# Loading the rows for the norm statistics two steps ahead of their squares, into the shared working tiles

## The chip, the cores and the metric

The kernel runs on one core of a Trainium2 chip. A core has five engines that run side by side, each through its own list of instructions in order: TensorE (matmuls; PE in the profile, its weight loads PEld), VectorE (DVE), ScalarE (ACT), GpSimd (POOL) and SyncE (SP), which here does little but issue DMAs. They wait for one another by semaphores. The metric is the time of one execution on the device in microseconds.

## The reference

The reference is one layer of a bidirectional encoder over 256 tokens of width 2048, in float32. Cut to what matters here:

```python
def rmsnorm(x, g):
    xf = x.astype(jnp.float32)
    y = xf * lax.rsqrt(jnp.mean(jnp.square(xf), axis=-1, keepdims=True) + EPS)
    return (y * g.astype(jnp.float32)).astype(x.dtype)
...
h = rmsnorm(x, norm_mix_g[l])
proj = h @ w_in[l]
...
qa = rmsnorm(split_heads(na_q, NA_HEADS), na_q_norm_g[l]) * (NA_HEAD_DIM ** -0.5)
...
mkv = rmsnorm(mem, mem_norm_g[l]) @ w_mem_kv[l]
```

Neighbourhood attention, retention and cross-attention into `mem` follow, each branch goes through a matrix of its own, the gated sum through `w_out`, and a squared-ReLU MLP ends the layer. The two norms of `x` and of `mem` need, for each token, the sum of the squares of its 2048 values.

## The kernel before

The work is a list of *units*. A unit is one tile of weights of 512 KB (two blocks of 128 rows, 512 columns) with its twelve matmuls of 512 columns: two blocks of rows, two halves of the tokens, and three products each (lines 101 to 103), since every operand is split into a high part and a low part that together carry float32. Eight units make a chunk of 512 output columns for `w_in`; the first three chunks are q and k of two head pairs twice, and v, then comes the same for the other heads, then the chunks of `w_mem_kv`.

For unit i the weights are loaded by SP into `raw` (line 242; five buffers, issued four units ahead), split by ScalarE into `w_hi` (line 94) and by VectorE into `w_lo` (line 95; four buffers each, split two units ahead in the program's text), and multiplied. For the first eight units the same happens to the transposed input: a load of `xT` into `xt_in` (line 160), and pieces `hT_hi` and `hT_lo` (lines 97 and 98).

The input is multiplied without the norm's factor, and the factor `r_x` is put in when a chunk is finished. So the statistics run beside the chunks, as a task: `stats_task` (line 167) loads the rows of `x`, 128 tokens by 512 columns (256 KB) at a time into `x_in`, and ScalarE squares them in place and leaves the sums in `ss` (line 175). After eight such blocks VectorE reduces `ss` (line 177), GpSimd raises to the power of -1/2 (lines 144 and 145), and VectorE makes one refining step (lines 146 to 149). The task for `x` is spawned at the start, that for `mem` (factor `r_m`) at unit 20.

`x_in` has a buffer of its own, one of it. Most other pieces of work take turns in twelve buffers of 2 KB per partition, the tag `t2`: `xt_in`, `qraw` (a finished chunk of q and k, copied from PSUM by ScalarE, line 300), `junk` (its squares, line 308), `na_bias`, `sb` (softmax rows), `pT`.

Behind `r_x` come, in this order: the squares of `qraw` on ScalarE (line 308), their sums on VectorE (line 309), the power on GpSimd, the normalising of `qraw` on VectorE (lines 320 and 322), its transposes on TensorE (line 287), and their split into `na_qkT` (lines 97 and 98). An attention head then makes scores `ps`, adds the bias and takes the maximum (line 379), exponentiates on ScalarE (line 357), scales (line 360), transposes (line 347) and multiplies by v.

The order on each engine is set by the tile framework's scheduler when the program is built. A buffer's next writer waits for its last reader; an instruction that waits holds up all behind it on its engine, and a DMA that waits holds up all behind it on SP.

Of the kernel before, what the change touches and what calls it, by code (L numbers as in the profile page):

```python
# [12 lines left out]
F32 = mybir.dt.float32  # L13
# [5 lines left out]
P = 128  # L19
D = 2048  # L20
S = 256
NT = S // P
KT = D // P
CW = 512
# [33 lines left out]
def encoder_layer(ctx: ExitStack, tc: tile.TileContext, a, out):  # L58
# [5 lines left out]
    wk = ctx.enter_context(tc.tile_pool(name="wk", bufs=12))  # L64
# [40 lines left out]
    def t2(name, dt=F32):  # L105

        return wk.tile([P, NT, S], dt, name=name, tag="t2")

    def t2f(name):
        return t2(name).rearrange("p t s -> p (t s)")  # L110
# [27 lines left out]
    def rsqrt_mean(ss, n, count, dst=None):  # L138

        u = st.tile([P, 8], F32, name="rs_u")  # L140
        y0 = st.tile([P, 8], F32, name="rs_y0")
        t = st.tile([P, 8], F32, name="rs_t")
        y = st.tile([P, 8], F32, name="rs_y") if dst is None else dst
        nc.gpsimd.tensor_scalar(u[:, :n], ss, 1.0 / count, EPS, op0=ALU.mult, op1=ALU.add)
        nc.gpsimd.tensor_tensor(y0[:, :n], u[:, :n], neg_half[:, :n], op=ALU.pow)
        nc.vector.tensor_tensor(t[:, :n], y0[:, :n], y0[:, :n], op=ALU.mult)
        nc.vector.tensor_tensor(t[:, :n], t[:, :n], u[:, :n], op=ALU.mult)
        nc.vector.tensor_scalar(t[:, :n], t[:, :n], -0.5, 1.5, op0=ALU.mult, op1=ALU.add)
        nc.vector.tensor_tensor(y[:, :n], y0[:, :n], t[:, :n], op=ALU.mult)
        return y  # L150
# [16 lines left out]
    def stats_task(src, dst):  # L167
        nh = D // CW
        ss = const.tile([P, NT, nh], F32, name=f"ss_{src.tensor.name}")
        for h in range(nh):  # L170
            for t in range(NT):
                xx = wk.tile([P, CW], F32, name="x_in", bufs=1)
                nc.sync.dma_start(xx, src[t * P:(t + 1) * P, h * CW:(h + 1) * CW])
                yield
                nc.scalar.activation(xx, xx, AF.Square, accum_out=ss[:, t, h:h + 1])
        s2 = st.tile([P, NT], F32, name="s2")
        nc.vector.tensor_reduce(s2, ss, axis=AX.X, op=ALU.add)
        rsqrt_mean(s2, NT, D, dst)
# [47 lines left out]
    raws, splits, x_in = {}, {}, []  # L226
# [301 lines left out]

    spawn(consts_task())
    spawn(stats_task(a["x"], r_x))  # L530

    memT = Lhs("memT")
# [392 lines left out]
    for i in range(n_units):  # L925
        issue(i + LOADS)
        do_split(i + SPLITS)
        for j in range(i, min(i + LEAD + 1, n_units)):
            if isinstance(units[j], Product):
                for lead, fn in units[j].acts:  # L930
                    if lead == j - i:
                        fn()
        if i == 20:
            spawn(stats_task(a["mem"], r_m))
        if i == 28:
            spawn(mem_task())
        if i == 100:
            spawn(decay_task())
        if i == u_out - 4:
            for c in range(4):  # L940
                env["x1", c] = quad_f("x1")
                nc.gpsimd.dma_start(env["x1", c],
                                    a["x"][:, c * CW:(c + 1) * CW].rearrange("(t p) d -> p t d", p=P))
        do_mm(i)
        units_done.append(i)
        run_tasks(i)
    i = n_units
# [105 lines left out]
```

## Time and profile before

| | |
|---|---|
| time, median of 3 runs | 1843.16 us (1839.11 to 1846.07) |
| the profiled execution's own time | 1837.19 us |
| its span, first to last instruction | 1835.4 us |
| TensorE busy | 1803.3 us, 98% of the span |
| VectorE busy | 1258.2 us, 69% |
| ScalarE busy | 977.5 us, 53% |
| GpSimd busy | 107.0 us, 6% |
| granted TensorE clock | 0.998 |
| bytes moved | 381.75 MB, 208 GB/s in the mean |

The durations below come from the one profiled execution, and all starts count from the start of its span. Busy time of TensorE is time with a matmul in flight; a matmul of 512 columns is shown as some 0.39 us long while the next one starts 0.23 us after it.

### The profile page before, as it was taken

The numbers are of one execution on the slowest core, as the hardware profiler recorded it, in microseconds if no ns is written. First come the engines' busy times: TensorE is split into PE (matmuls) and PEld (weight loads), VectorE is DVE, ScalarE is ACT, GpSimd is POOL, SyncE is SP. The second block draws the span as 40 slices with busy tenths as digits, with TensorE's granted clock in tenths as the row PEclk, the third lists the DMA queues.
The fourth block names the chain that finished last, engine by engine and source line by source line (L and its number), as shares of the span: only waits on it lengthen the run. The fifth ranks groups of instructions, "written<-read, shape, count | busy, mean of one in ns | idle before, by whom it ended". The sixth has DMA issues, their size and how long they took to land.

```text
span 1835.4 us, 22408 instructions
## 1 busy us (share of the span) xinstructions
PE 1803.3 (98%) x8248; PEld 1489.9 (81%) x8248; DVE 1258.2 (69%) x1608; ACT 977.5 (53%) x1222; POOL 107.0 (6%) x120
## 2 busy tenths in 40 slices
PE   8999999999999999999999999998999999999999
PEld 6778888888888888888888888776888887888887
DVE  5678766745454575675655555787888878888884
ACT  6566555544444444444444445955565656666562
POOL 0101010000000000000000000011101111110100
PEclk9999999999999999999999999999999999999999
DMA  8776455455555555545565555697888798979764
GB/s 269 261 228 209 161 173 172 164 193 194 195 189 198 188 170 185 172 162 195 187 213 197 193 184 183 197 258 209 243 261 237 239 269 233 260 242 273 212 208 144
DMA packets 131581, 381.75 MB, mean 208 GB/s; under 512 B 12176, under 2 KB 12688, under 8 KB 131472
## 3 DMA queue, kind: packets, MB, share of 16 engines
q1 hardware_dynamic: 114736, 346.07, 55.0%
q0 software_dynamic: 16448, 33.56, 10.1%
q8 instruction: 64, 1.05, 0.2%
q10 hardware_dynamic: 288, 0.70, 0.1%
q14 instruction: 45, 0.37, 0.1%
HBM read 378.19 MB, written 2.10 MB: 207 GB/s over the span
## 4 chain that ended last, share of the span: by engine, by line
PE 80%; DMA 10%; DVE 4%; ACT 3%; issue 2%; POOL 0%; SPq 0%; ACTq 0%; DVEq 0%; POOLq 0%
PE acc L102 23%; PE acc L101 23%; PE acc L103 23%; DMA b<-in_w_ff 6%; DVE w_lo L95 3%; PE ps L103 2%; PE ps L101 2%; PE ps L102 2%; ACT w_hi L94 2%; DMA x_in<-in_mem 2%; DMA x_in<-in_x 1%; DMA raw<-in_w_ff 1%; PE pt L103 1%; PE pt L101 1%; PE pt L102 1%
## 5 line engine op out<-in xcount | busy, mean ns | idle before, releaser
L95 DVE TENSOR_TENSOR w_lo<-raw,w_hi 128x1024 fp32r<-128x1024 f32 (+1 forms) x585 | 711.3, 1221 | 408.4 <-ACT w_hi L94 406.4
L94 ACT ACTIVATE w_hi<-raw 128x1024 fp32r<-128x1024 f32 (+1 forms) x585 | 616.2, 1057 | 540.8 <-PE acc L103 481.4
L101 PE MATMUL acc<-w_hi,hT_hi 128*128 128x512 f32 x1024 | 403.4, 394 | 7.1 <-ACT hT_hi L97 4.9
L102 PE MATMUL acc<-w_lo,hT_hi 128*128 128x512 f32 x1024 | 400.4, 391 | 4.5 <-DVE w_lo L95 4.5
L103 PE MATMUL acc<-w_hi,hT_lo 128*128 128x512 f32 x1024 | 399.7, 390 | 0.0
L94 ACT ACTIVATE w_hi<-b 128x1024 fp32r<-128x1024 f32 x140 | 148.1, 1062 | 175.0 <-DMA b<-in_w_ff 57.8
L101 PEld LDWEIGHTS acc<-w_hi,hT_hi 128*128 128x128 f32 x1024 | 192.9, 188 | 46.5 <-ACT hT_hi L97 4.9
L102 PEld LDWEIGHTS acc<-w_lo,hT_hi 128*128 128x128 f32 x1024 | 192.8, 188 | 44.8 <-DVE w_lo L95 6.8
L103 PEld LDWEIGHTS acc<-w_hi,hT_lo 128*128 128x128 f32 x1024 | 192.6, 188 | 40.7
L95 DVE TENSOR_TENSOR w_lo<-b,w_hi 128x1024 fp32r<-128x1024 f32 x140 | 169.5, 1222 | 78.0 <-ACT w_hi L94 76.7
L102 PE MATMUL acc<-w_lo,fT_hi 128*128 128x512 f32 x512 | 200.0, 391 | 2.4 <-DVE w_lo L95 2.4
L101 PE MATMUL acc<-w_hi,fT_hi 128*128 128x512 f32 x512 | 200.4, 391 | 0.3 <-DVE x L773 0.3
L103 PE MATMUL acc<-w_hi,fT_lo 128*128 128x512 f32 x512 | 199.4, 390 | 0.0
L102 PEld LDWEIGHTS acc<-w_lo,fT_hi 128*128 128x128 f32 x512 | 96.2, 188 | 23.9 <-DVE w_lo L95 4.3
L101 PEld LDWEIGHTS acc<-w_hi,fT_hi 128*128 128x128 f32 x512 | 96.3, 188 | 20.4 <-issue 0.7
L103 PEld LDWEIGHTS acc<-w_hi,fT_lo 128*128 128x128 f32 x512 | 96.2, 188 | 20.0
L819 POOL DMA_DIRECT2D b<-in_w_ff x56 | 68.1, 1363 | 549.1 <-DVE b L823 196.0
L101 PE MATMUL acc<-w_hi,memT_hi 128*128 128x512 f32 x128 | 50.8, 397 | 0.0
L101 PE MATMUL acc<-w_hi,mT_hi 128*128 128x512 f32 x128 | 50.6, 395 | 0.0
L102 PE MATMUL acc<-w_lo,memT_hi 128*128 128x512 f32 x128 | 50.0, 390 | 0.0
L103 PE MATMUL acc<-w_hi,memT_lo 128*128 128x512 f32 x128 | 50.0, 390 | 0.0
L103 PE MATMUL acc<-w_hi,mT_lo 128*128 128x512 f32 x128 | 49.9, 390 | 0.0
(266 smaller groups left out, 2439.2 us busy)
## 6 DMA issues: line engine op xcount, KB each, us to landing
raw<-in_w_in SPq DMA_DIRECT2D x255, 512.0 KB, 3.3
raw<-in_w_ff SPq DMA_DIRECT2D x200, 512.0 KB, 5.9
b<-in_w_ff SPq DMA_DIRECT2D x56, 512.0 KB, 7.0
b<-in_w_ff POOLq DMA_DIRECT2D x56, 512.0 KB, 8.9
raw<-in_w_mem_kv SPq DMA_DIRECT2D x32, 512.0 KB, 3.2
raw<-in_w_br_ret SPq DMA_DIRECT2D x32, 512.0 KB, 3.4
raw<-in_w_out SPq DMA_DIRECT2D x32, 512.0 KB, 3.2
raw<-in_w_br_na SPq DMA_DIRECT2D x16, 512.0 KB, 3.2
```

The costliest lines, as they stand in the source:

```text
L94: nc.scalar.activation(hi, src, AF.Copy)
L95: nc.vector.tensor_tensor(lo, src, f(hi), op=ALU.subtract)
L101: nc.tensor.matmul(o, lhsT=lh, rhs=rh, start=start, stop=False)
L102: nc.tensor.matmul(o, lhsT=lh, rhs=rl, start=False, stop=False)
L103: nc.tensor.matmul(o, lhsT=ll, rhs=rh, start=False, stop=stop)
L819: nc.gpsimd.dma_start(ring[n][k % 2].rearrange("p (b c) -> p b c", b=2), src, accum_op=ALU.add)
```

## The change

In `stats_task`, the blocks no longer go through a tile of their own but through the shared working tiles `t2`, and the square of a block is put two steps behind its load: at each step the next block is loaded, and the block of two steps ago is squared.

```diff
@@ -167,12 +167,17 @@
     def stats_task(src, dst):
         nh = D // CW
         ss = const.tile([P, NT, nh], F32, name=f"ss_{src.tensor.name}")
-        for h in range(nh):
-            for t in range(NT):
-                xx = wk.tile([P, CW], F32, name="x_in", bufs=1)
+        held = []
+        for i in range(nh * NT + 2):
+            if i < nh * NT:
+                h, t = i // NT, i % NT
+                xx = t2f("x_in")
                 nc.sync.dma_start(xx, src[t * P:(t + 1) * P, h * CW:(h + 1) * CW])
-                yield
+                held.append((xx, t, h))
+            if i >= 2:
+                xx, t, h = held.pop(0)
                 nc.scalar.activation(xx, xx, AF.Square, accum_out=ss[:, t, h:h + 1])
+            yield
         s2 = st.tile([P, NT], F32, name="s2")
         nc.vector.tensor_reduce(s2, ss, axis=AX.X, op=ALU.add)
         rsqrt_mean(s2, NT, D, dst)
```

All lines behind line 178 move down by five. With the scheduler the change moves instructions on every engine up to about unit 60; behind that the order is the same. TensorE's order is the same up to unit 36, but for the matmuls of unit 7 among themselves. Three places:

On SP, the loads of the first units, from the load of xT for unit 4 on, with what each waits for (DMAHW is an earlier DMA, Activation is ScalarE, DVE is VectorE). Before:

```order
L160 DMA xt_in<-in_xT 128x512 [waits DMAHW4_49]
L173 DMA x_in<-in_x 128x512 [waits DMAHW5_49]
L242 DMA raw<-in_w_in 128x1024 [waits DMAHW6_49,DVE_49]
L160 DMA xt_in<-in_xT 128x512 [waits DMAHW7_49]
L242 DMA raw<-in_w_in 128x1024 [waits DMAHW0_49,DVE_49]
L173 DMA x_in<-in_x 128x512 [waits DMAHW1_49,Activation_49]
L160 DMA xt_in<-in_xT 128x512 [waits DMAHW2_49]
L242 DMA raw<-in_w_in 128x1024 [waits DMAHW3_49,DVE_49]
L160 DMA xt_in<-in_xT 128x512 [waits DMAHW4_49]
L173 DMA x_in<-in_x 128x512 [waits DMAHW5_49,Activation_49]
```

And now:

```order
L160 DMA xt_in<-in_xT 128x512 [waits DMAHW4_49]
L175 DMA x_in<-in_x 128x512 [waits DMAHW5_49]
L247 DMA raw<-in_w_in 128x1024 [waits DMAHW6_49,DVE_49]
L160 DMA xt_in<-in_xT 128x512 [waits DMAHW7_49]
L175 DMA x_in<-in_x 128x512 [waits DMAHW0_49]
L247 DMA raw<-in_w_in 128x1024 [waits DMAHW1_49,DVE_49]
L160 DMA xt_in<-in_xT 128x512 [waits DMAHW2_49]
L175 DMA x_in<-in_x 128x512 [waits DMAHW3_49]
L247 DMA raw<-in_w_in 128x1024 [waits DMAHW4_49,DVE_49]
L160 DMA xt_in<-in_xT 128x512 [waits DMAHW5_49]
```

Each load of x now has no wait for ScalarE, and one stands with every weight load instead of every second one.

On VectorE, the first reduction of the statistics, counted from the last piece of hT (unit 7). Before, `x9` being nine splits in a row:

```order
L98 SCALAR_TENSOR_TENSOR hT_lo<-xt_in,c_gains,hT_hi 128x256 x2
L95 TENSOR_TENSOR w_lo<-raw,w_hi 128x1024 x9
L177 TENSOR_REDUCE s_370<-ss_in_x 128x2
L146 TENSOR_TENSOR rs_t<-rs_y_373 128x2
L147 TENSOR_TENSOR rs_t<-rs_t,rs_u 128x2
L148 TENSOR_SCALAR rs_t<-rs_t 128x2
L149 TENSOR_TENSOR r_x<-rs_y_373,rs_t 128x2
L95 TENSOR_TENSOR w_lo<-raw,w_hi 128x1024
L309 TENSOR_REDUCE ssq<-junk 128x4 x2
```

And now:

```order
L98 SCALAR_TENSOR_TENSOR hT_lo<-xt_in,c_gains,hT_hi 128x256 x2
L95 TENSOR_TENSOR w_lo<-raw,w_hi 128x1024 x4
L182 TENSOR_REDUCE s_406<-ss_in_x 128x2
L146 TENSOR_TENSOR rs_t<-rs_y_409 128x2
L147 TENSOR_TENSOR rs_t<-rs_t,rs_u 128x2
L148 TENSOR_SCALAR rs_t<-rs_t 128x2
L149 TENSOR_TENSOR r_x<-rs_y_409,rs_t 128x2
L77 COPY c_tables<-r_x 128x1
L95 TENSOR_TENSOR w_lo<-raw,w_hi 128x1024
L314 TENSOR_REDUCE ssq<-junk 128x4 x2
L95 TENSOR_TENSOR w_lo<-raw,w_hi 128x1024
L146 TENSOR_TENSOR rs_t<-rs_y_500 128x8
```

The reduction moved up by five units: it stands ahead of the split of unit 12 instead of unit 17, and the normalising behind it ahead of unit 14 instead of unit 19.

On VectorE, the reduction for mem. Before, the split behind it is that of unit 31:

```order
L95 TENSOR_TENSOR w_lo<-raw,w_hi 128x1024 x4
L98 SCALAR_TENSOR_TENSOR na_qkT_lo<-pt,c_gains,na_qkT_hi 128x2x128
L177 TENSOR_REDUCE s_868<-ss_in_mem 128x2
L146 TENSOR_TENSOR rs_t<-rs_y_871 128x2
L98 SCALAR_TENSOR_TENSOR na_qkT_lo<-pt,c_gains,na_qkT_hi 128x2x128
L147 TENSOR_TENSOR rs_t<-rs_t,rs_u 128x2
L148 TENSOR_SCALAR rs_t<-rs_t 128x2
L149 TENSOR_TENSOR r_m<-rs_y_871,rs_t 128x2
L95 TENSOR_TENSOR w_lo<-raw,w_hi 128x1024
```

And now, where the split behind it is that of unit 25:

```order
L95 TENSOR_TENSOR w_lo<-raw,w_hi 128x1024
L182 TENSOR_REDUCE s_931<-ss_in_mem 128x2
L146 TENSOR_TENSOR rs_t<-rs_y_934 128x2
L147 TENSOR_TENSOR rs_t<-rs_t,rs_u 128x2
L148 TENSOR_SCALAR rs_t<-rs_t 128x2
L149 TENSOR_TENSOR r_m<-rs_y_934,rs_t 128x2
L95 TENSOR_TENSOR w_lo<-raw,w_hi 128x1024 x2
L98 SCALAR_TENSOR_TENSOR v_lo<-acc_543,r_x,v_hi 128x512
```

The eight loads for mem follow on SP the weight loads of units 23 to 27 in ones and twos, where before they were spread over those of units 23 to 33.

## Rows read from the trace of the kernel before

**Rows 1.** Windows: stretch, length, PE, PEld, DVE, ACT, POOL busy, clock, DMA share, GB/s.

```profile
0.00:10.00 10.00, 3.31 (x6) 1.98 (x7) 3.83 (x18) 4.76 (x9) 0.68 (x6) 1.00 0.74 229
10.00:20.00 10.00, 10.00 (x42) 8.15 (x41) 9.83 (x21) 9.36 (x17) 0.00 (x0) 1.00 0.94 355
20.00:30.00 10.00, 10.00 (x45) 8.28 (x45) 6.25 (x10) 5.71 (x11) 0.00 (x0) 1.00 0.86 272
10.00:150.00 140.00, 132.77 (x611) 108.23 (x610) 95.59 (x186) 90.21 (x158) 15.76 (x19) 1.00 0.76 253
```

**Rows 2.** Tile x_in, its landing times; then SP's own waits to 110 us.

```profile
DMA to landing us min/median/max: 3.1/4.1/7.3
...
SPq L173 <- ACT x_in L175: 38.7, 13, 4.5
```

**Rows 3.** TensorE's timeline: start, duration us, line, operation [idle before it <-releaser].

```profile
47.71 0.39 PE L102 MATMUL acc<-w_lo,hT_hi 128*128 128x512 f32 x1
...
55.64 0.39 PE L101 MATMUL acc<-w_hi,hT_hi 128*128 128x512 f32 x1
57.51 0.50 PE L102 MATMUL acc<-w_lo,hT_hi 128*128 128x512 f32 x1 [1.48 <-DVE w_lo L95]
57.85 0.40 PE L103 MATMUL acc<-w_hi,hT_lo 128*128 128x512 f32 x1
...
65.34 0.50 PE L102 MATMUL acc<-w_lo,hT_hi 128*128 128x512 f32 x1 [0.78 <-DVE w_lo L95]
...
101.09 0.39 PE L103 MATMUL acc<-w_hi,hT_lo 128*128 128x512 f32 x1
...
104.38 0.39 PE L103 MATMUL acc<-w_hi,hT_lo 128*128 128x512 f32 x1
...
110.10 0.40 PE L102 MATMUL acc<-w_lo,hT_hi 128*128 128x512 f32 x1
```

**Rows 4.** TensorE's timeline where nothing waits: transposes, scores, transposes with scores between.

```profile
67.72 0.39 PE L103 MATMUL acc<-w_hi,hT_lo 128*128 128x512 f32 x1
...
68.62 0.40 PE L102 MATMUL acc<-w_lo,hT_hi 128*128 128x512 f32 x1
...
94.91 0.39 PE L103 MATMUL acc<-w_hi,hT_lo 128*128 128x512 f32 x1
...
96.08 0.40 PE L102 MATMUL acc<-w_lo,hT_hi 128*128 128x512 f32 x1
...
118.57 0.39 PE L103 MATMUL acc<-w_hi,hT_lo 128*128 128x512 f32 x1
...
120.18 0.40 PE L102 MATMUL acc<-w_lo,hT_hi 128*128 128x512 f32 x1
```

**Rows 5.** VectorE's timeline: the two reductions of the statistics, two weight splits.

```profile
54.26 0.16 DVE L177 TENSOR_REDUCE s<-ss_in_x 128x2 f32<-128x8 f32 x1 [2.50 <-ACT x_in L175]
...
56.23 1.23 DVE L95 TENSOR_TENSOR w_lo<-raw,w_hi 128x1024 fp32r<-128x1024 f32 x1
...
58.66 1.23 DVE L95 TENSOR_TENSOR w_lo<-raw,w_hi 128x1024 fp32r<-128x1024 f32 x1
...
100.57 0.16 DVE L177 TENSOR_REDUCE s<-ss_in_mem 128x2 f32<-128x8 f32 x1 [2.08 <-ACT x_in L175]
```

**Rows 6.** GpSimd's timeline at the first two normalisings of q and k.

```profile
58.73 1.21 POOL L144 TENSOR_SCALAR rs_u<-ssq 128x8 f32<-128x8 f32 x1 [3.21 <-DVE c_tables L77]
60.02 1.65 POOL L145 TENSOR_TENSOR rs_y<-rs_u,neg_half 128x8 f32<-128x8 f32 x1
...
67.70 0.20 POOL L144 TENSOR_SCALAR rs_u<-ssq 128x8 f32<-128x8 f32 x1 [4.73 <-DVE ssq L309]
```

**Rows 7.** ScalarE's timeline at unit 4: split, pieces of hT, first square.

```profile
14.93 1.06 ACT L94 ACTIVATE w_hi<-raw 128x1024 fp32r<-128x1024 f32 x1 [0.19 <-DMA raw<-in_w_in]
15.89 0.89 ACT L97 ACTIVATE hT_hi<-xt_in,c_gains 128x256 fp32r<-128x256 f32 x2
16.69 0.62 ACT L175 ACTIVATE x_in<-x_in 128x512 f32<-128x512 f32 x1
```

## Prediction

> **What bounds the kernel now.** I read the windows first, then TensorE's own timeline, and then, from its stalls back, the engines that feed it. The windows [rows 1] say that from 10 to 150 us TensorE has matmuls in flight for 132.77 of 140 us, so 7.2 us are open idle time, and that the DMA engines are nearly full only between 10 and 20 us (0.94 of their time, 355 GB/s). The timeline of TensorE tells what a stall costs in full. A unit is one 512 KB weight tile, twelve matmuls of 512 columns; undisturbed they start 0.2266 us apart (35 steps from 47.71 to 55.64) [rows 3], so a unit takes 2.72 us. A stall also delays the starts around it, so I count starts: from the first matmul of unit 17 (units counted from 0) at 55.64 to the second of unit 32 at 110.10 are 181 steps [rows 3], worth 41.02 us. Between them stand four blocks of four transposes, one block of scores, and one of transposes with scores. Undisturbed, the three kinds add 0.45 us (67.72 to 68.62, less two steps), 0.72 (94.91 to 96.08) and 1.16 (118.57 to 120.18) [rows 4]; together 1.79 + 0.72 + 1.16 = 3.67. So the stretch needs 44.69 us and took 54.46: **9.77 us are lost there**. Before unit 17 the starts show no gap, and the stretch up to 150 us after unit 32 has no wait of TensorE.
>
> Perfetto Trace Analysis, section Identifying the Most-Contended Engine, in the Trainium skill says that matmul busy time is a poor measure since pipelined matmuls look different in a trace. The two counts here bear it out (7.2 by busy time, 9.77 by starts); by busy time the sum below would be 2.6 us smaller.
>
> Where the loss comes from: one tile holds every row block of x_in, so the load of the next waits on SP until ScalarE has squared the last: 13 waits, 38.7 us together [rows 2]. Landing takes 3.1 to 7.3 us, 4.1 in the middle [rows 2]; with the square this makes some 5 us a block and 40 for eight. So the sum of x is only reduced at 54.26, after VectorE has waited 2.50 us, and r_x holds up the split of unit 17 until 56.23 [rows 5]. VectorE works in order, and TensorE pays: from 55.64 to 57.85 are 2.21 us for two steps, 1.76 lost. The same at 100.57 for mem, where VectorE waited 2.08 [rows 5]: from 101.09 to 104.38 are 3.29 for three steps, 2.61 lost [rows 3]. The other 5.4 us are what follows: r_x late makes the normalising of q and k late, and transposes and splits behind it stall around 63 to 66 (the restart at 65.34 is one [rows 3]), 74 and 89; mem's squares make the first head's softmax late at 106 to 109.
>
> **The change, part by part.** Nothing is added or removed in work: 16 loads of 256 KB, 16 squares, the same reductions. Only waits and order move.
>
> *Loads of x.* Their wait on ScalarE goes; each now follows one weight load, so all eight are issued by the time that unit 7 is split, not one per 5 us. Behind them on SP stand the weight loads, which in the kernel before stood behind blocked x loads. What can it cost? The engines must land 256 KB more per unit just where they are fullest. Count bytes in the order of issue: all up to the weights of unit 12 (13 weight tiles, 8 blocks of xT, 8 of x, the gains) are 11.05 MB. By 20 us, 2.29 + 3.55 = 5.84 MB had moved [rows 1]; the other 5.21 take 14.7 us at 355 GB/s, or 19.2 at the 272 of the next window [rows 1]. So unit 12 is there at 34.7 or 39.2, is split about 2.3 us later (ScalarE 1.06, VectorE 1.23 [rows 5, 7]), and is wanted at 55.64 - 5 x 2.72 = 42.0. Units 6 and 7 are landed near 20 and 23 and wanted at 25.7 and 28.4. Cost: nothing at either rate, with 0.5 us to spare at the worse one.
>
> *Squares of x.* Per unit ScalarE then has a split (0.96 from start to start), two pieces of hT (0.80) [rows 7] and a square, 0.62 and the read of its sum, 0.8 at most: 2.56 us against TensorE's 2.72. It keeps up. Its last x squares stand behind the two copies of the first finished chunk, which cannot start before unit 7 ends at 31.1. Two copies, three squares and two splits, each at 0.8 to 0.96, end near 37. Then reduction to the end of the next split as before (54.26 to 57.46, 3.2 us [rows 5]): unit 12 is split by 40.2 and wanted at 42.0. **The 1.76 us go**, with 1.8 us of cover.
>
> *The q/k normalising behind r_x.* r_x is there at about 38.9 and not 56.2. From r_x (the split starts at 56.23) to GpSimd's start at 58.73 are 2.5 us; its two instructions take 1.21 + 1.65; from their end to TensorE's restart at 65.34 are 3.7 [rows 3, 5, 6]. So the split of unit 14, which now stands behind this piece, is through at 38.9 + 2.5 + 2.86 + 3.7 = 48.0; it is wanted at 47.7. A stall of 0.3, with the late restart 0.4 to 0.5. The second time the first instruction took only 0.20 [rows 6]; then the split is through at 47.0 and nothing stalls. Here a weight split comes next on VectorE and runs at that moment, as one did at 58.66 [rows 5], so I take the longer: **0.5 us new**. Everything behind, the transposes before units 19 and 20 first, has then some 15 us of cover: they no longer stall.
>
> SBUF — State Buffer, section Who interferes with whom, in the Trainium skill says that a VectorE instruction with two SBUF inputs contends with a GpSimd instruction that reads SBUF. The 1.21 beside a split and the 0.20 without one agree; by that rule the 0.5 is paid, without it the forecast would be 0.5 us lower.
>
> *Loads and squares of mem.* The loads are issued from about 53 us, in ones and twos between weight loads, each some two units ahead of its square; ScalarE may wait 1 to 3 us for a landing of 4 to 7 us. By then the splits run three units ahead of TensorE (a split's buffer is freed four units back), about 8 us less 2.3 for the split itself. The reduction of mem now stands before unit 25's split and not unit 31's. I reckon r_m near 74 us and unit 25 split near 75.5, wanted at 78: **the 2.61 us go**, and with ScalarE free of mem's squares the softmax of the first head is done some 4 us before its transposes. With that the whole 5.4 goes too.
>
> *Shared tiles.* The 16 blocks now take turns with xt_in, qraw, junk and the heads in twelve buffers. In the order no x_in load waits for more than an earlier DMA; the later loads of memT wait for TensorE three times, against four before. No cost taken; up to 1 us either way. From unit 36 the heads' matmuls are spread one head every three units where two heads came together before; that stretch had no waits and I take none, bounded by 1 us.
>
> **Sum:** -9.77 + 0.5 = -9.3 us against the profiled execution, 1837.19 to 1827.9. The median of the runs shown is 5.97 us (0.3%) above that execution; with this difference kept the forecast is 1833.9, taken as **1834**. What is won before 110 us stays: later, loads and splits are released by TensorE's own progress.
>
> **Rivals.** (a) Only the two statistics stalls go, 1.76 + 2.61 = 4.4, since the transposes and the softmax were held by something else (an issue limit of TensorE, ScalarE's waits for mem now packed into fewer units): 1838.8. For it: the windows between 60 and 90 show VectorE and ScalarE busy with other pieces too; against it: all those pieces follow r_x or mem's squares in order. (b) No effect: the shared tiles make the loads wait for other readers, so that the change doesn't do what it says, or the waits move to new places of equal size: 1843. Against it: the waits named in the order. (c) Slower: the x loads crowd out the weights between 12 and 40 us. It starts to cost where the engines bring less than 5.21 MB in the 19.7 us that leave time to split unit 12, 264 GB/s; 272 was the rate next to it, when loads were blocked for part of the time. It undoes the whole gain below 5.21 / 29 = 180 GB/s, and at 140 GB/s TensorE loses 17.5 us: about 8 us slower than before, 1851. Against it: 355 GB/s when loads were queued.
>
> **How the numbers follow.** The forecast (all of it, -8 to -10.3): 0.66. (a): 0.20. (b): 0.09. (c): 0.05. One half of a percent is 9.2 us here, about what a measurement of this kernel can tell from no change, and the forecast lies just on it: of its 0.66 I put 0.42 beyond. So faster 0.42, within 0.53, slower 0.05. The range goes from the full 10.3 less some scatter of the runs, 1831, to (a) and a little above it, 1842.
>
> **What would show it.** Right: x_in loads all issued by about 25 us; the reduction of x on VectorE near 37, of mem near 72; TensorE's waits from 10 to 130 us under 1 us, the one left at unit 14; the second matmul of unit 32 near 100.8. The first step is wrong if weights land late between 20 and 40 us and TensorE waits there for splits; the third if waits for w_lo, qraw or sb remain between 60 and 110; the last if new waits show between 110 and 190. The forecast fails if what is won by 110 us is not there at the end.

## The result, and the profile after the change

The changed kernel takes 1827.26 us (median of 4 runs, 1826.15 to 1828.45), the kernel before 1842.01 us (4 runs beside it, 1839.11 to 1846.07). The ratio is 0.9923, with a 95% interval from 0.9904 to 0.9941: 0.77% faster, beyond the half percent. The forecast had the direction and the mechanism, but was 1834, and its range, 1831 to 1842, ends above the measured time.

Yet the profiled execution agrees with it: 1828.31 us, span 1826.5, which is 8.9 below that of the kernel before, where 9.3 were forecast. So the question for the experiments is not where the stalls went but why the runs differ by more than the profiles.

The windows of the changed kernel, columns as in [rows 1]:

```profile
10.00:20.00 10.00, 10.00 (x37) 8.09 (x36) 9.93 (x20) 9.29 (x19) 0.00 (x0) 1.00 1.04 405
20.00:30.00 10.00, 10.00 (x46) 8.26 (x44) 6.91 (x10) 7.64 (x14) 0.00 (x0) 1.00 1.04 401
10.00:150.00 140.00, 140.00 (x648) 116.59 (x647) 102.81 (x193) 94.36 (x162) 17.23 (x20) 1.00 0.74 260
```

TensorE has a matmul in flight for all of the 140 us, where [rows 1] had 132.77. The DMA engines bring 405 and 401 GB/s where they brought 355 and 272: the loads of x now stand in the queue instead of waiting for squares.

The tile x_in: its squares, its loads with first and last issue, who waits, its landing times. It answers [rows 2].

```profile
L179 ACT ACTIVATE x_in<-x_in x16: 616/623/634, 16.5 to 73.7; 128x512 f32<-128x512 f32 x16
...
L175 SPq DMA_DIRECT2D x_in<-in_x x8: 327/328/328, 8.7 to 23.9; - x8
L175 SPq DMA_DIRECT2D x_in<-in_mem x8: 419/437/1075, 54.0 to 67.0; - x8
...
  ACT x_in L179: 5.4, 4
...
DMA to landing us min/median/max: 5.0/6.6/8.2
```

All loads of x are issued by 23.9 us. A landing takes longer than before (6.6 against 4.1 us in the middle), and it matters no more, because several are under way at once. SP's 13 waits of 38.7 us for the square are gone; what is left is 5.4 us in which ScalarE waits for blocks of mem.

VectorE's two reductions (start, duration, line, operation [idle before it <- releaser]), which answer [rows 5]:

```profile
37.13 0.15 DVE L182 TENSOR_REDUCE s<-ss_in_x 128x2 f32<-128x8 f32 x1
...
74.41 0.16 DVE L182 TENSOR_REDUCE s<-ss_in_mem 128x2 f32<-128x8 f32 x1 [0.15 <-ACT x_in L179]
```

And TensorE at the first matmul of unit 17 and the first two of unit 32, which answer [rows 3]:

```profile
56.52 0.39 PE L101 MATMUL acc<-w_hi,hT_hi 128*128 128x512 f32 x1
...
101.14 0.39 PE L101 MATMUL acc<-w_hi,hT_hi 128*128 128x512 f32 x1
101.37 0.39 PE L102 MATMUL acc<-w_lo,hT_hi 128*128 128x512 f32 x1
```

From 56.52 to 101.37 are 44.85 us; 54.46 were needed before, and the undisturbed starts were reckoned at 44.69. So 9.6 of the 9.77 lost microseconds are back. TensorE reached unit 17 itself 0.88 us later than before (56.52 against 55.64), and 9.6 less 0.9 is the 8.7 that the two executions differ by at unit 32.

### The profile page after: what moved, and what is told of

Read it like the earlier page. It is cut to its first block, busy times and chain, and to the rows that moved or that the text cites. A ratio compares the mean times of both kernels' runs of the same rounds, so it can differ in the third digit from the quotient of the medians.

```text
span 1826.5 us, 22386 instructions
## 1 busy us (share of the span) xinstructions
PE 1803.5 (99%) x8248; PEld 1492.6 (82%) x8248; DVE 1258.5 (69%) x1608; ACT 976.3 (53%) x1222; POOL 107.2 (6%) x120
## 3 DMA queue, kind: packets, MB, share of 16 engines
q8 instruction: 64, 1.05, 0.2%
## 4 chain that ended last, share of the span: by engine, by line
PE 81%; DMA 7%; DVE 5%; ACT 4%; issue 2%; SPq 0%; ACTq 0%; DVEq 0%; POOL 0%; POOLq 0%
PE acc L101 24%; PE acc L102 24%; PE acc L103 24%; DMA b<-in_w_ff 6%; DVE w_lo L95 3%; ACT w_hi L94 2%; PE ps L102 2%; PE ps L101 2%; PE ps L103 2%; DMA raw<-in_w_ff 1%; PE pt L292 1%; PE pt L103 1%; PE pt L102 1%; PE pt L101 1%; DVE b L828 1%
## 5 line engine op out<-in xcount | busy, mean ns | idle before, releaser
L102 PEld LDWEIGHTS acc<-w_lo,hT_hi 128*128 128x128 f32 x1024 | 193.2, 189 | 38.7 <-DVE w_lo L95 0.4
```

The source lines that it names most:

```text
L102: nc.tensor.matmul(o, lhsT=lh, rhs=rl, start=False, stop=False)
```

## Experiments

Below, "the stretch" is the time from TensorE's first matmul of unit 17 to its first of unit 32, and "the late part" is from there to the end of the span. The stretch is 109.87 - 55.64 = 54.23 us in the first profile of the kernel before; the late part is 1835.4 - 109.87 = 1725.5.

### Both kernels again

The kernel before, without an edit:

> The kernel before, unchanged, profiled and timed a second time, to see whether the 5 us by which its runs lay above its profiled execution belong to it. T1 (the serial chain of load and square sets TensorE's stalls, and the landing times on it differ from one execution to the next): the runs scatter over 5 us or more again, the medians stay near 1842, and the second profile shows another length of the stretch from the first matmul of unit 17 to the second of unit 32 (54.46 us in the first) by 1 us or more, with the x_in waits on SP changed by about as much. T2 (the excess lies elsewhere, in the start or behind 150 us, or was an accident of few runs): that stretch is again 54.5 within 0.5 us; what differs between the profiles lies before 10 or behind 150 us, or the median comes down to about 1838.

It took 1841.93 us (12 runs, 1835.32 to 1848.23); 24 runs beside it 1841.54 (1834.16 to 1846.82); ratio 1.0004 [0.9988, 1.002]. So this kernel scatters over 14 us, and its first profiled execution, 1837.19, stood among the shortest: of all 79 runs of it in this study 10 were as short. The second profiled execution took 1843.58. What lies between the two: unit 17 begins 0.9 later, the stretch is 54.97, 0.7 longer, and the late part is 1730.3, 4.8 longer. In the late part ScalarE waits for blocks of `b` in the feed-forward part, which a plain load fills and an accumulating one adds to; where the accumulating loads are left out, below, these waits are gone. Here they are, first in the kernel before and then in its second profile (engine, line, what it waited for: us in total, times, longest):

```profile
ACT w_hi L94 <- DMA b<-in_w_ff: 57.8, 18, 9.2
```

```profile
ACT w_hi L94 <- DMA b<-in_w_ff: 67.2, 18, 7.2
```

That is mostly T2, with a part of T1: the stretch did change, by 0.7 us.

The changed kernel, also without an edit:

> The changed kernel, unchanged, profiled and timed a second time beside new runs of the kernel before. The first timing had four runs of it, within 2.3 us of one another, at the height of its profiled execution. In the two profiles of the kernel before, taken apart by the starts of GpSimd's instructions, the second is 6.4 us longer: 0.9 from the start, 0.7 from the stalls between units 17 and 32, the other 4.8 behind 1150 us, where the accumulating loads of b land. T2 (the excess of before's runs over its first profile comes mostly from the late stretch, which the change does not touch, so the changed kernel has it too and its four runs were low by chance): more runs scatter over 6 us or more, median 1829 to 1832, 10 to 12.5 below before. T1 (the excess comes from the statistics' chains and went with them): median 1826 to 1828 again, scatter under 4 us, 14 to 15.5 below before.

It took 1831.85 us (6 runs, 1826.24 to 1835.33), the kernel before beside it 1841.62 (11 runs); ratio 0.9939 [0.9915, 0.9963]. The stretch was 44.63 us, the late part 1729.8, against 1725.4 in the first profile of the changed kernel. So the changed kernel scatters as well, over 9 us, and in the place that T2 named. T1, that the scatter went with the chains, falls.

> The changed kernel once more. With the accumulating loads left out the change is worth 10.0 us in the runs; with them the first timing gave 14.75 (four runs of it) and the second 9.8 (six). T2 (the gain is 9 to 10.5 and the four first runs were low by chance out of a scatter of 9 us): the median lies at 1830 to 1833 again, 9 to 12 below the runs of before beside it. T5 (the change also shortens the late stretch in the mean, by shifting when its loads begin): 1826 to 1829, 13 or more below.

This time 1827.56 us (5 runs, 1825.46 to 1830.98) against 1841.83 (17 runs); ratio 0.9926 [0.9905, 0.9947]. By the numbers put down, that speaks for T5 and against T2, while the run before spoke for T2. Once more:

> The changed kernel once more beside the last one, for the number of its runs: 15 so far, mean 1828.9, against 68 of the kernel before, mean 1841.6, so 12.7 less with about 1.8 either way, while the pair without accumulating loads gave 10.3 less (means) with about 1.4. T2 (the late stretch is the same in the mean and the rest is chance): these runs lie at a mean of 1830 to 1833. T5 (the late stretch is some 2 us shorter with the change): at 1827 to 1829.

1828.42 us (6 runs, 1826.06 to 1833.81; mean 1829.0) against 1839.87 (11 runs); ratio 0.994 [0.9923, 0.9956]. The mean lies at the upper end of what T5 named and 1 us below what T2 named, so it doesn't part them either. All runs together: 21 of the changed kernel, median 1828.28, mean 1828.9, from 1825.46 to 1835.33; 79 of the kernel before, median 1841.09, mean 1841.4, from 1832.96 to 1850.41. The means differ by 12.5 us, with 1.5 either way (1.96 standard errors). The first four runs of the changed kernel were 1 us below what 21 show.

### The late part made quiet

In both kernels the accumulating loads are left out:

```diff
         def ring_add(n, k, src):
-            nc.gpsimd.dma_start(ring[n][k % 2].rearrange("p (b c) -> p b c", b=2), src, accum_op=ALU.add)
+            pass
```

> The kernel before with the accumulating loads of b in the feed-forward part left out (line 819: the second summand never arrives, so its result is left incomplete), to take away the late landings that differ from one execution to the next. Up to 1150 us nothing changes. T2: shorter late stretch, and a scatter of the runs under 3 us, nearly all of it from the start and the stalls between 55 and 110 us. T1: scatter of 5 us or more as before, since the chains are still there. The difference to its companion with the change is what the change saves without the late stretch: by the profiles so far 8.7 to 10.3 us; by T1 13 or more.

> The changed kernel with the same accumulating loads of b left out (its result in the feed-forward part is incomplete in the same way). T2: 8.7 to 10.3 us below its companion without the change, scatter under 2 us. T1: 13 us or more below it, with a much narrower scatter than its companion's.

Without the change 1819.43 us (6 runs, 1818.05 to 1822.42), with it 1809.39 (6 runs, 1808.43 to 1810.26). Both scatters shrink: beside these runs the two whole kernels had 14.3 us (11 runs) and 9.1 (6 runs), here it is 4.4 and 1.8 (6 runs each), so most of the scatter comes from these loads (T2). The difference is 10.0 us by the medians and 10.3 by the means, with 1.3 either way by the same rule, or 1.6 with the wider factor that so few runs ask for; T1 wanted 13. In the profiles the stretch is 53.78 and 44.63, the late part 1706.6 and 1706.9: what the change wins is won in the stretch, and nothing comes or goes behind it.

What is left of the scatter, 4.4 us against 1.8, fits the statistics' stalls, though six runs each prove little. In all five profiles of the changed kernel the stretch is 44.62 or 44.63; in the three of the kernel before it is 53.78 (with the accumulating loads left out), 54.23 and 54.97. The clock looks like a reason. The windows around the restart after mem's stall, first in the kernel before, then in its second profile (columns as in [rows 1]):

```profile
104.00:106.00 2.00, 1.96 (x9) 1.61 (x10) 1.46 (x5) 1.42 (x2) 0.00 (x0) 1.00 0.83 236
```

```profile
106.00:108.00 2.00, 2.00 (x6) 1.52 (x6) 1.47 (x7) 1.63 (x3) 0.00 (x0) 0.50 0.75 236
108.00:110.00 2.00, 2.00 (x9) 1.56 (x7) 2.00 (x6) 1.35 (x5) 0.00 (x0) 0.74 0.65 236
```

TensorE had waited 1.65 us for w_lo in both. In the one it went on at the full 2.4 GHz, in the other at 0.50 of it, which is 1.2 GHz, and its matmuls started 0.43 us apart instead of 0.23. Its timeline from there to unit 32, first in the kernel before, then in the second profile:

```profile
104.04 0.50 PE L102 MATMUL acc<-w_lo,hT_hi 128*128 128x512 f32 x1 [1.65 <-DVE w_lo L95]
...
107.90 0.41 PE L347 MATMUL pt<-ident,sb 128*128 128x128 f32 x2 [1.07 <-DVE sb L360]
108.88 0.44 PE L347 MATMUL pt<-ident,sb 128*128 128x128 f32 x2 [0.56 <-DVE sb L360]
...
109.87 0.40 PE L101 MATMUL acc<-w_hi,hT_hi 128*128 128x512 f32 x1
```

```profile
103.50 0.50 PE L101 MATMUL acc<-w_hi,hT_hi 128*128 128x512 f32 x1 [0.86 <-ACT w_hi L94]
105.64 0.80 PE L102 MATMUL acc<-w_lo,hT_hi 128*128 128x512 f32 x1 [1.65 <-DVE w_lo L95]
106.24 0.63 PE L103 MATMUL acc<-w_hi,hT_lo 128*128 128x512 f32 x1
106.67 0.63 PE L101 MATMUL acc<-w_hi,hT_hi 128*128 128x512 f32 x1
...
110.48 0.44 PE L347 MATMUL pt<-ident,sb 128*128 128x128 f32 x2 [0.26 <-DVE sb L360]
...
111.47 0.39 PE L101 MATMUL acc<-w_hi,hT_hi 128*128 128x512 f32 x1
```

From 105.64 to 108.80 it made seven steps in 3.16 us, where the first profile took 1.73. Yet this cost nothing: from the restart to unit 32 are 5.83 us in both, since the transposes behind these matmuls wait for the softmax `sb`, 1.07 and 0.56 us in the first profile and only 0.26 in the second. In the kernel before without accumulating loads the clock fell too, to 0.50 from 106 to 108 us; the 5.83 us are the same there (103.89 to 109.72), and its stretch is the shortest of the three. So the three stretches differ ahead of mem's reduction: from unit 17 to it are 44.48, 44.93 and 45.67 us, with 17.5, 18.0 and 19.6 us in which ScalarE waited for blocks of mem to land. The landing times go with the difference; the clock does not.

### Each half alone

The new loop for one of the two statistics, the old one with its single tile for the other:

```diff
+        if dst is r_x:
+            held = []
+            for i in range(nh * NT + 2):
...
+        else:
             for h in range(nh):
                 for t in range(NT):
                     xx = wk.tile([P, CW], F32, name="x_in", bufs=1)
```

> Only the statistics of x are loaded two steps ahead into the shared tiles; those of mem keep the single tile. Counted by starts, of the 9.77 us that the kernel before loses between units 17 and 32 some 5.1 lie before the start of mem's stall and 4.65 behind it. T1 (each chain costs what the trace shows, and the runs' scatter comes from the chains): about 5 us less in the profile, 1832; in the runs 5 to 8 less than before, and a scatter about half of before's. T2 (scatter and excess have nothing to do with the chains): 5 less in both, the scatter as before. T3 (the softmax and the transposes behind 85 us hang on r_x too, or mem's chain simply becomes the later one): the gain is under 3 us since mem's stall grows by what was won.

> Only the statistics of mem are loaded two steps ahead into the shared tiles; those of x keep the single tile. T1: mem's stall of 2.61 us, the 2.04 at the first softmax go, 4.65 together: 1832.5 in the profile, in the runs 4.5 to 8 below before, about half of its scatter left; TensorE's stall at unit 17 stays (2 us). T2: 4.65 in both, scatter as before. T3: under 3 us, since the pieces held by r_x late come to stand where mem's did.

Only x ahead: 1833.29 us (7 runs), 8.3 below the 1841.54 beside it; ratio 0.9951 [0.9931, 0.997]. Only mem ahead: 1838.3 us (12 runs), 3.2 below; 0.998 [0.9965, 0.9996]. In the profiles the stretch is 46.81 and 50.73, so x alone brings 7.4 of the 9.6 us and mem alone 3.5. T1 gave them 5.1 and 4.65. The sum is more than the whole, so the parts overlap, and the direction is the contrary of T3: with x ahead, mem's stall grows smaller by itself. The scatters, 6.9 us in 7 runs and 10.1 in 12 against 12.7 in the 24 beside them, decide nothing between T1 and T2. Here is mem's reduction with only x ahead:

```profile
90.74 0.16 DVE L190 TENSOR_REDUCE s<-ss_in_mem 128x2 f32<-128x8 f32 x1 [4.11 <-ACT x_in L188]
```

and the loads of mem in the kernel before and with only x ahead (first and last issue behind the colon):

```profile
L173 SPq DMA_DIRECT2D x_in<-in_mem x8: 327/328/423, 60.3 to 95.9; - x8
```

```profile
L186 SPq DMA_DIRECT2D x_in<-in_mem x8: 328/328/582, 43.9 to 84.5; - x8
```

The chain of mem is still serial, but it begins at 43.9 us instead of 60.3 (its first load now stands five weight loads earlier in SP's order), its last load is issued at 84.5 instead of 95.9, and its sum comes at 90.74 instead of 100.57. TensorE now waits 1.07 us for the weights behind it, where 1.65 and what follows were lost. So a good part of what the prediction booked under mem was a consequence of x. With only mem ahead, unit 17 still waits for r_x, 1.77 us.

### Which part of the edit does it

The old loop, load and square in turn, but through the shared tiles:

```diff
-                xx = wk.tile([P, CW], F32, name="x_in", bufs=1)
+                xx = t2f("x_in")
```

> The loop of before, load then square, but the block goes through the shared working tiles and not through a tile of its own: one half of the change, without the two steps. T1 (the single buffer made the chain; how far the square stands behind the load in the text hardly matters, since SP issues loads as soon as nothing blocks it): within 2 us of the changed kernel, 1826 to 1829; the reductions stand at the same places in VectorE's order. T4 (the two steps are what brings it: with a square right behind its load ScalarE waits some 4 to 5 us for each landing, in order ahead of the splits of weights): ScalarE's waits for x_in from DMA 30 us or more, TensorE stalls in 20 to 40 us, and half of the gain or more is gone, 1834 to 1842.

1830.3 us (6 runs, 1826.76 to 1835.58), 11.2 below; ratio 0.9944 [0.9922, 0.9966]. That is 2.0 above the 1828.28 of the changed kernel, just outside the 1826 to 1829 of T1, with some 3 us either way. The stretch is 44.63 us, the same as in the changed kernel to the hundredth, and the loads are issued within 0.3 us of the same times:

```profile
L173 SPq DMA_DIRECT2D x_in<-in_x x8: 327/328/328, 8.8 to 24.2; - x8
L173 SPq DMA_DIRECT2D x_in<-in_mem x8: 418/432/794, 53.7 to 66.9; - x8
...
  ACT x_in L175: 5.4, 6
```

So the two steps in the text do nothing that can be seen; more than one buffer is what did it (T1's first sentence; T4's waits of ScalarE are 5.4 us, not 30). SP runs ahead as soon as no buffer blocks it.

Two tiles of its own instead of one, and eleven shared ones instead of twelve, so that the pool keeps its size:

```diff
-    wk = ctx.enter_context(tc.tile_pool(name="wk", bufs=12))
+    wk = ctx.enter_context(tc.tile_pool(name="wk", bufs=11))
...
-                xx = wk.tile([P, CW], F32, name="x_in", bufs=1)
+                xx = wk.tile([P, CW], F32, name="x_in", bufs=2)
```

> The loop of before, but x_in has two tiles of its own instead of one, and the shared tiles are eleven instead of twelve, since the memory is full. Theory (the serial chain of one buffer set the stalls; a block took some 5 us for load and square where TensorE takes 2.72 us a unit): with two a block comes every 2.5 us, the reduction of x on VectorE falls from 54.3 to 36 to 42, TensorE has under 1 us of waits between 20 and 130 us, and the runs are within 2 us of the changed kernel's, 9 to 11 below before. Rival (more than two must be in flight, or the shared tiles miss the twelfth): x_in waits on SP of 15 us or more hold up weights behind them, TensorE loses 3 us or more between units 12 and 32, and the runs lie 4 to 7 below before.

1834.14 us (12 runs, 1830.91 to 1839.33), 7.7 below; ratio 0.9963 [0.9947, 0.9979]. Two buffers bring the stretch to 44.63 as well, but lose 4 us ahead of it: unit 17 begins at 59.99. VectorE reduces the sums of x at 39.13, not at 35.9 to 37.1 as in the changed kernel's profiles, and then this happens to unit 14 (TensorE's timeline, and the window behind it):

```profile
48.01 0.39 PE L101 MATMUL acc<-w_hi,hT_hi 128*128 128x512 f32 x1
50.29 0.50 PE L102 MATMUL acc<-w_lo,hT_hi 128*128 128x512 f32 x1 [1.89 <-DVE w_lo L95]
50.62 0.40 PE L103 MATMUL acc<-w_hi,hT_lo 128*128 128x512 f32 x1
```

```profile
52.00:54.00 2.00, 2.00 (x6) 1.62 (x5) 1.64 (x2) 0.00 (x0) 0.00 (x0) 0.50 0.83 295
```

A wait of 1.89 us, and behind it the 1.2 GHz level until 54.5. From 50.29 to 54.50 are eleven steps in 4.21 us, 1.7 more than at 0.2266 each; no wait stands behind them here that could take this up, and unit 17 is later by both. This is the stall that the prediction put at unit 14. It is real; in the changed kernel it is missed by half a microsecond. The outcome is nearer to the rival's: SP still waited 18.1 us for squares, and TensorE lost 3.8 us at unit 14. Whether the missing twelfth tile has a part in it was not tried.

### A version that beats both

Since the late part was found to hang on the accumulating loads, I gave one of them more time: product m7 of the round before goes behind m6, so that one more unit lies between the split that frees `b2` and the split that needs it. The first run of it left the load of `b2` eight units ahead, where two loads overwrite a block that m7 has still to read, so its feed-forward part is another computation:

> The changed kernel with one other edit in the late stretch: product m7 of the round before is put behind m6 instead of ahead of it, so that the accumulating load of b2 has six units instead of five between the split that frees it and the split that needs it. If ScalarE's waits for b from DMA (33 us in 9 in the profile of the changed kernel) end last there, they fall by half or more and the runs fall by 3 to 8 us, with less scatter. Rival (the load of b2 for the next round then waits longer on SP and holds up the loads behind it, or the queue of accumulating loads is what limits): within 1.5 us of the changed kernel's, or slower.

1824.74 us (5 runs). With the load six units ahead it stands behind that read:

```diff
-            return Product(mm, [(8, lambda: ring_load("b2", k, w2[NK + k])),
+            return Product(mm, [(6, lambda: ring_load("b2", k, w2[NK + k])),
...
-            out_units += [m3(k), m5(k)] + ([m7(k - 1)] if k else []) + [m6(k), m2(k), m4(k)]
+            out_units += [m3(k), m5(k), m6(k)] + ([m7(k - 1)] if k else []) + [m2(k), m4(k)]
```

> The changed kernel with product m7 of the round before behind m6, as in the run before, and the load of b2 six units ahead instead of eight, so that it stands behind the split of m7 (in the run before, two of the loads of b2 overwrote a block that m7 had still to read, so its feed-forward part was wrong). If it is the landing of the accumulating loads that ScalarE waits for in the late stretch, its waits for b from DMA fall by half and the runs lie 2 to 5 us below the changed kernel's, at 1824 to 1827, with a scatter under 5 us. Rival (the loads of b2, now later, are waited for in their place): 1828 or more, scatter as before.

1822.25 us (6 runs, 1820.93 to 1824.18), 17.6 below the kernel before, ratio 0.9904 [0.989, 0.9917], and 6.2 below the 1828.42 of the changed kernel beside it; the scatter is 3.3 us. But the reason that I gave is not seen: ScalarE's waits for `b` from DMA did not fall by half. In the changed kernel's last profile and in this one they are

```profile
ACT w_hi L94 <- DMA b<-in_w_ff: 56.6, 16, 8.2
```

```profile
ACT w_hi L94 <- DMA b<-in_w_ff: 54.0, 20, 6.8
```

What did fall is their share of the chain of work that ended last, from 6 or 7% of the span in the changed kernel's profiles to 3%, and TensorE's own waits behind 150 us, from 13.3 us to 10.4 in these two profiles. So the waits for `b` still happen, and it may be that fewer of them set TensorE's time. The two profiled executions are only 3.0 us apart, though, and the rest of the 6.2 is not explained.

## Why the prediction was right and wrong

**The bound and the stalls: right.** The serial load and square of x_in cost 9.77 us between units 17 and 32 by starts; 9.6 came back. TensorE has no wait between 20 and 130 us.

**Loads of x: right, on the cautious side.** Issued by 23.9 us, reduction at 37.13 (forecast 25 and 37), mem's at 74.41 (forecast near 72). No weights came late, and the engines brought over 400 GB/s where I took 355 as the most; rival (c) had no ground.

**Unit 14: the work was reckoned right, the stall did not come.** From r_x to the end of unit 14's split I had 9.06 us, from 38.9 to 48.0; it was 8.9, from 39.16 to 48.09 (the split begins at 46.93 and takes 1.16). GpSimd's first instruction took the long time, beside a split, in every profile of the changed kernel; here its row, as in [rows 6]:

```profile
41.78 1.10 POOL L144 TENSOR_SCALAR rs_u<-ssq 128x8 f32<-128x8 f32 x1 [3.41 <-DVE ssq L314]
```

SBUF — State Buffer, section Who interferes with whom, in the Trainium skill says that a VectorE instruction with two SBUF inputs contends with a GpSimd instruction that reads SBUF. The 1.10 agrees, against the 0.20 of the row without a split beside it: the split ran from 41.60 to 42.82, and GpSimd's instruction ended at 42.88.

But TensorE wanted that split at 48.58 in this execution, since it had started later; in another (unit 17 at 55.74, close to the kernel before) the sums of x were reduced at 36.35 and the split was through at 47.3, wanted at 47.8. So the term of 0.5 is zero, with half a microsecond of cover, and the run with two tiles of its own shows that 2 us later it is a stall of 1.9, with 1.7 from the clock on top.

**The parts of the 9.77: wrong between themselves.** x's chain alone is worth 7.4, not the 5.1 that I read from the starts, because with it out of the way mem's loads are issued 10 to 16 us earlier too. The sum is the same.

**Shared tiles and the heads' new order: nothing, as taken.** The late part is 1706.6 and 1706.9 in the quiet pair.

**From the profile to the runs: the step that failed.** "With this difference kept" I added the 5.97 us by which the median of three runs lay above the profiled execution, and then took a range of some scatter around one number. But these 5.97 were no constant of the kernel. They were one draw, of a profiled execution in the lowest eighth, from a kernel that scatters over 17 us. In the changed kernel the same term measured -1.05: its four runs have a median of 1827.26, its profiled execution took 1828.31 (against all 21 runs it is 0.0). Without the term the forecast would have been the 1827.9 of the sum.

Against the larger number of runs the miss of 6.6 us (1833.9 to 1827.26) splits up by medians so: 2.1, since the median of three runs, 1843.16, was above that of 79, 1841.09; 1.0, since four runs of the changed kernel lay below 21 of them, 1828.28; and 3.5, since the gain is 12.8 by medians and not 9.3. Of the 3.5, 0.8 are the quiet pair's 10.0 against 9.3: 0.5 is the term of unit 14, which cost nothing, and the rest is less than that pair can tell from chance.

**Open.** The rest is 12.5 against 10.3 by the means: 2.2 us, with 2.0 to 2.2 either way. Either it is chance, or with the change the late part is some 2 us shorter when the accumulating loads are there; the cause of this part stays open. Its length is 1725.4, 1729.8, 1726.1 and 1725.2 in four profiles of the changed kernel, 1725.5 and 1730.3 in two of the kernel before; that doesn't decide it.

**What the trace had to say on it beforehand.** The chain of work that ended last, in the page of the kernel before, names the landing of `b` with 6% of the span, some 110 us, and of x_in with 3%. Work that hangs on landings for over 100 us did scatter from execution to execution here, and seven microseconds between three runs said the same. The working held two forecasts 6 us apart, 1827.9 by the profiled execution and 1833.9 by the median, and the range should have reached below the lower one. Its low end was instead the full 10.3 below the median, less some 2 us of scatter.

## What to carry to other kernels

A chain that goes through one buffer (load, use, load) is loosened by a second one and cut by more (SP's waits were 38.7 us with one, 18.1 with two, none with the shared tiles), and it pays off to look for the chain in the order of the queue: a blocked load also holds back the loads of the next task behind it. Before a forecast is made from one profiled execution, see where that execution stands among the runs shown; if the runs scatter by more than the gain, forecast the difference, and give the scatter of the medians on both sides to the range. Where a stall is missed by half a microsecond, as at unit 14, it is not gone: a change that comes 2 us later pays it. What a slower clock behind a stall costs depends on what follows: 1.7 us at unit 14, nothing at 106 us, where the next wait took it up.

## What was not expected of the hardware

The DMA engines brought 405 and 401 GB/s over two windows of 10 us, where the kernel before had 355 at most in such a window. After waits of the same 1.65 us TensorE went on at 1.2 GHz in one execution and at 2.4 in another; in a third it started at 2.4 and fell to 1.2 about 1 us later. And at the start of the changed kernel its matmuls stood 0.43 us apart until 13.75 us, though the granted clock is given as 1.00 there:

```profile
12.90 0.63 PE L101 MATMUL acc<-w_hi,hT_hi 128*128 128x512 f32 x1
13.33 0.63 PE L103 MATMUL acc<-w_hi,hT_lo 128*128 128x512 f32 x1
13.75 0.52 PE L102 MATMUL acc<-w_lo,hT_hi 128*128 128x512 f32 x1
14.11 0.40 PE L103 MATMUL acc<-w_hi,hT_lo 128*128 128x512 f32 x1
14.35 0.39 PE L101 MATMUL acc<-w_hi,hT_hi 128*128 128x512 f32 x1
```

In the kernel before this ended at 11.36 us. That is where the 0.88 us at unit 17 come from: at the tenth start the changed kernel was 0.59 us ahead (10.77 against 11.36), at the nineteenth 0.87 behind (14.35 against 13.48). In thirteen profiles (all but that with two tiles of its own) unit 17 began between 55.0 and 57.2 us, those with the old loop for x among the others. The spacing is the one that the granted clock of 0.50 goes with above; why the clock reads 1.00 there, the rows don't tell.
